# Low parts of weights over the raw tiles in place, 2048 columns at once, with other scheduling priorities

## The chip, the cores and the metric

The kernel runs on one core of one Trainium2 chip. The metric is the device time of one execution in microseconds (us); the time of a kernel is the median of several runs. The engines are named as in the profile: PE (TensorE, matmuls; PEld is its weight load), DVE (VectorE), ACT (ScalarE), POOL (GpSimd) and SP (SyncE, which issues most DMAs).

## The reference

One layer of a hybrid trunk for 256 positions and a model width of 2048, all in fp32. A normalised input is projected 13312 columns wide; the columns feed three branches of width 1024 (a spatial-gating MLP, an S5 state-space layer with a GLU, and a cross-attention into 256 memory rows) and three sets of merge gates.

```python
def hybrid_layer(x, mem, ...):
    h = rms_norm(x, pre_g)
    proj = h @ w_in
    a_u, a_v, a_g, b_x, b_g, x_q, x_g, gate_logits = jnp.split(proj, splits, axis=-1)
    y_a = spatial_gating(a_u, a_v, sg_ln_g, sg_ln_b, sg_w, sg_b) * jax.nn.silu(a_g)
    y_b = s5_branch(b_x, a_re, a_im, log_dt, b_re, b_im, c_re, c_im, d, glu_w, glu_b) * jax.nn.silu(b_g)
    y_x = memory_cross_attention(x_q, rms_norm(mem, mem_g), xa_wk, xa_wv) * jax.nn.silu(x_g)
    ys = jnp.stack([y_a, y_b, y_x], axis=2)
    branch = jnp.einsum('bsnc,ncd->bsnd', ys, w_branch)
    gates = jax.nn.sigmoid(gate_logits.reshape(bsz, seq, N_BRANCH, D_MODEL))
    merged = jnp.sum(gates * branch, axis=2)
    out = merged @ w_out
    return x + rms_norm(out, post_g)
```

## The kernel before

**Weights.** All large products go through PE in fp32r, with each fp32 number split in two: a high part (the number cast to fp32r) and a low part (what is left of it). A product is then high·high, low·high and high·low. The weights come as 160 blocks of 128 x 2048 fp32, 1 MB each. `load` (L76) issues one DMA on SP into a tile of the pool `rawp`, which has three. `split` (L85) takes half a block, 1024 columns: `halves` (L81) gives it one of four tiles of the pool `hip`, with room for 1024 high and 1024 low columns, and `split_to` (L91) has ACT cast the high part (L92) and DVE subtract it from the raw numbers (L93). So a block takes two casts and two subtractions, and its raw tile is free when the second subtraction is done.

**Matmuls.** `cm_mm` (L172) holds the weights stationary and gives channel-major results: for each 128 columns of a block one matmul of 512 columns with the high part (L175) and one of 256 with the low part (L174; L177 for the first of a group, behind the high one). `tm_mm` (L179 to L182) moves the weights, 512 columns at a time, three matmuls each (high, low, high). `cm_block` (L210) and `tm_quarter` (L218) run one block, `cm_pairs` (L234) runs blocks in pairs into one PSUM tile of the pool `accp`.

**Stages.** The first eight pieces of `start` (L250 to L272) hold x transposed and the first 512 columns of w_bx; then come four w_bx blocks of the S5 branch, the queries (w_xq), the memory's keys and values (wk, wv), the gates of the branches, and `merge` (L780), which runs for each branch over four column groups: four blocks of w_gate, a sigmoid into a tile `sg` of the pool `wk` (L785), two blocks of w_br. The GLU (L910 to L925) multiplies four blocks and writes `yB`, which the S5 branch's merge reads. `w_out` and `w_out3` (L977 to L1019) project the result; L1024 to L1042 normalise, add the residual and write `y_out`. The last `w_out3` block's first half is split into tiles of the pool `s5p`.

**What sets the order.** PE runs in program order, written out by hand. ACT, DVE, POOL and SP are ordered by the scheduler of the framework by priority, which falls in program order; `tc.high_priority(offset=n)` moves what is issued inside it n places ahead. Splits, and the normalisation of memT (`mem_half`), go ahead by AHEAD = 250. After every half block `pump` (L186) lets small background generators run on: those of `bg[2]` (`rms_row` L290, attention, layer norm and the like) a step each, and the S5 layer's main one (`bg[0]`) by credits. Their steps have BEHIND = 0, no shift. In `rms_row` the row factors are turned into a broadcast `bc_x` through a diagonal tile `dg` (L305), a matmul (L312) and an ACT copy (L315), and then multiplied onto the tiles U and X (L330). `fold_u` (L341) adds the two halves of a PSUM tile into U or X with an ACT copy (L342) and a DVE addition (L343). In attention the scores `sc` (L717) are reduced (L722, L723), turned into exponentials `p` on ACT (L726), scaled on DVE (L730, L732) and transposed on PE (`tp`, L738). The S5 layer's products and scans are L374 and L606, its small exponent tables `E` are built at L377.

Of the kernel before, what the change touches and what calls it, by code (L numbers as in the profile page):

```python
# [18 lines left out]
P = 128  # L19
# [11 lines left out]
PI2_2 = 0.0019340515136718750  # L31
PI2_3 = 2.0 * math.pi - PI2_1 - PI2_2
RND = 12582912.0
AHEAD = 250
BEHIND = 0
NWARM = 8
CM_OFF = 352 // 4
RT = (0.66, 0.8, 0.47, 0.62, 0.58, 0.55, 1.32)
GELU_S = 2.0 * math.sqrt(2.0 / math.pi)
GELU_C = 0.044715  # L40
# [3 lines left out]
def trunk(ctx: ExitStack, tc: tile.TileContext, I, out):  # L44
    nc = tc.nc
    v, a, g, pe = nc.vector, nc.scalar, nc.gpsimd, nc.tensor

    xp = ctx.enter_context(tc.tile_pool(name="xp", bufs=1))
    xv = xp.tile([P, T + 48], F32, name="xv")
    const = ctx.enter_context(tc.tile_pool(name="const", bufs=1))  # L50
    big = ctx.enter_context(tc.tile_pool(name="big", bufs=1))
    rawp = ctx.enter_context(tc.tile_pool(name="rawp", bufs=3))
    hip = ctx.enter_context(tc.tile_pool(name="hip", bufs=4))
    wk = ctx.enter_context(tc.tile_pool(name="wk", bufs=2))
    s5p = ctx.enter_context(tc.tile_pool(name="s5p", bufs=2))
    s5c = ctx.enter_context(tc.tile_pool(name="s5c", bufs=1))
# [19 lines left out]
    def load(src):  # L76
        t = rawp.tile([P, 2048], F32, tag="raw", name=nm("raw"))
        nc.sync.dma_start(out=t, in_=src)
        return t

    def halves(off):  # L81
        t = hip.tile([P, 2 * 1024 + 128], F32R, tag="hl", name=nm("hl"))
        return t[:, off:off + 1024], t[:, off + 1024:off + 2048]

    def split(src, off=0):  # L85
        hi, lo = halves(off)
        with tc.high_priority(offset=AHEAD):
            split_to(hi, lo, src)
        return hi, lo

    def split_to(hi, lo, src):  # L91
# [116 lines left out]
    rate = {"cm": 0.62, "tm": RT[6]}  # L208

    def cm_block(ps, raw, hl, mm_=cm_mm):  # L210
        for hf in range(2):
            wh, wl = split(raw[:, hf * 1024:(hf + 1) * 1024], CM_OFF)
            for k in range(8):
                kk = hf * 8 + k
                mm_(ps, wh[:, k * P:(k + 1) * P], wl[:, k * P:(k + 1) * P], hl[kk], kk == 0, kk == 15)
            pump(rate["cm"])

    def tm_quarter(acc, raw, hl, kq, nk):  # L218
        for hf in range(2):
            wh, wl = split(raw[:, hf * 1024:(hf + 1) * 1024])  # L220
            for k in range(2):
                kk = kq * 4 + hf * 2 + k
                sl = slice(k * 512, (k + 1) * 512)
                for tb in range(2):
                    tm_mm(acc[tb], wh[:, sl], wl[:, sl], hl[kk], tb, kk == 0, kk == nk - 1)
            pump(rate["tm"])
# [130 lines left out]
    cm_block(ps[:, 1], load(I["w_bx"][3]), xhl)  # L357
# [419 lines left out]
    def merge(n, yhl, sink):  # L777
        for c in range(4):
            rate["tm"] = RT[6] + (0.33, 0.13, 0.0, 0.0)[c] * (n == 2)
            G = acc_tile()  # L780
            for kq in range(4):
                tm_quarter([G[:, 0], G[:, 1]], load(I["w_gate"][n, c, kq]), xhl, kq, 16)
            assert not bg[2]
            Bp = acc_tile()
            sg = wk.tile([P, 2, 512], F32, tag="w0", name=nm("g"))  # L785
            for tb in range(2):
                a.activation(out=sg[:, tb], in_=G[:, tb], func=AF.Sigmoid, scale=rstd_x[:, tb:tb + 1])
            for kq in range(2):
                tm_quarter([Bp[:, 0], Bp[:, 1]], load(I["w_br"][n, c, kq]), yhl, kq, 8)
            sink(c, sg, Bp)  # L790
# [118 lines left out]
        yB += [s5p.tile([P, 2, T], F32R, tag=tag, name=nm("yB"), bufs=n) for _ in range(n)]  # L909
    for bp in range(4):  # L910
        ps = acc_tile()
        raw = load(I["glu"][bp])
        for b in range(2):
            wh, wl = split(raw[:, b * 1024:(b + 1) * 1024], CM_OFF)
            for k in range(8):
                cm_mm(ps[:, b], wh[:, k * P:(k + 1) * P], wl[:, k * P:(k + 1) * P], ygl[k], k == 0, k == 7)
        t = fold(ps, None)
        for i in range(2):
            a.activation(out=t[:, i, :], in_=t[:, i, :], func=AF.Sigmoid, bias=glu_b[:, 2 * bp + i:2 * bp + i + 1])
        b = slice(2 * bp, 2 * bp + 2)  # L920
        v.tensor_tensor(out=t, in0=t, in1=u[:, b, :], op=ALU.mult)
        v.tensor_tensor(out=t, in0=t, in1=sb[:, b, :], op=ALU.mult)
        for i in range(2):
            d = yB[2 * bp + i]
            split_to(d[:, 0], d[:, 1], t[:, i])  # L925
# [63 lines left out]

    acc = acc_tile()  # L990
    for kh in range(2):
        raw = load(I["w_out3"][0, kh])
        for hf in range(2):
            wh, wl = split(raw[:, hf * 1024:(hf + 1) * 1024])
            for k in range(4):
                for tb in range(2):
                    tm_k(acc[:, tb, 0:T], wh[:, k * T:(k + 1) * T], wl[:, k * T:(k + 1) * T], kh * 8 + hf * 4 + k, tb)
# [7 lines left out]

    wks = []
    for kh in range(2):
        raw = load(I["w_out3"][1, kh])
        for hf in range(2):
            src = raw[:, hf * 1024:(hf + 1) * 1024]  # L1010
            if kh == 0 and hf == 0:
                for i in range(2):
                    wh = s5p.tile([P, 512], F32R, tag="s", name=nm("wh"), bufs=4)
                    wl = s5p.tile([P, 512], F32R, tag="s", name=nm("wl"), bufs=4)
                    split_to(wh, wl, src[:, i * 512:(i + 1) * 512])
                    wks += [(wh[:, k * T:(k + 1) * T], wl[:, k * T:(k + 1) * T]) for k in range(2)]
            else:
                wh, wl = split(src)
                wks += [(wh[:, k * T:(k + 1) * T], wl[:, k * T:(k + 1) * T]) for k in range(4)]  # L1019
# [116 lines left out]
```

## Time and profile before

| | us |
|---|---|
| median of 3 runs | 913.08 |
| lowest, highest run | 912.48, 913.41 |
| the profiled execution | 913.93 |
| its span | 912.2 |
| DVE subtractions of splits (L93, 128x1024), 319 of 1220 ns | 388.1 |
| ACT casts of splits (L92, 128x1024), 319 of 1044 ns | 331.3 |

The profile is of one execution. Its page gives busy times by engine, and the trace behind it answers further views: what an engine waited for, a timeline of instructions with the idle time before each and what ended it, groups of instructions by line and form, and busy time in windows. A row of the timeline reads: start, duration, engine, line, operation, written tile <- read tiles, shape, count. Numbers of buffers are left out of names, so `hl` is any tile of `hip`, and `raw` any raw tile.

### The profile page before, as it was taken

How to read it: one execution, taken by the hardware profiler on the slowest of the kernel's cores; microseconds unless marked ns; L12 is line 12 of the kernel's file. 1: busy time of each engine (PE TensorE's matmuls, PEld its weight loads, DVE VectorE, ACT ScalarE, POOL GpSimd, SP SyncE). 2: the span in 40 equal slices, each digit the busy share in tenths (PEclk: the TensorE clock that was granted, in tenths of full speed). 3: DMA queues.
4: the chain of work that ended last, by engine and by line, in shares of the span. 5: the costliest groups of instructions: out<-in, count | busy, mean ns of one | idle time of the engine just before them, and what ended most of it. 6: DMA issues, size and time to landing. Idle time of an engine off the chain costs nothing.

```text
span 912.2 us, 12951 instructions
## 1 busy us (share of the span) xinstructions
PE 899.3 (99%) x4864; PEld 798.4 (88%) x4864; DVE 751.5 (82%) x1172; ACT 562.6 (62%) x962; POOL 49.8 (5%) x78
## 2 busy tenths in 40 slices
PE   8999999999999999999999999999999999999996
PEld 6999898889888888889989888889988889998896
DVE  6899967976779999899779998999889647876554
ACT  7585755855558677774456667767656546544452
POOL 1000000100001111110000010101000000000000
PEclk9999999999999999999999999999999999999999
DMA  9887665555455656665645656565655755557542
GB/s 337 312 311 294 226 231 194 202 193 191 154 205 176 242 187 227 231 212 207 231 167 186 221 203 212 190 213 203 231 190 194 258 195 203 211 185 277 194 175 93
DMA packets 32575, 195.30 MB, mean 214 GB/s; under 512 B 4224, under 2 KB 6528, under 8 KB 10752
## 3 DMA queue, kind: packets, MB, share of 16 engines
q1 hardware_dynamic: 28000, 186.08, 56.6%
q0 software_dynamic: 3936, 6.16, 3.1%
q10 hardware_dynamic: 576, 2.23, 0.6%
q8 instruction: 38, 0.62, 0.3%
q14 instruction: 25, 0.20, 0.1%
HBM read 190.39 MB, written 2.10 MB: 211 GB/s over the span
## 4 chain that ended last, share of the span: by engine, by line
PE 86%; DVE 9%; ACT 1%; DMA 1%; issue 1%; SPq 0%; DVEq 0%; ACTq 0%
PE acc L180 19%; PE acc L181 19%; PE acc L182 19%; PE acc L175 17%; PE acc L174 8%; DVE hl L93 4%; PE y L630 1%; ACT hl L92 1%; PE po L748 1%; DMA M<-memT 1%; DMA st<-start 1%; PE bu L568 1%; DVE q L374 1%; PE sc L717 1%; DVE tS L377 1%
## 5 line engine op out<-in xcount | busy, mean ns | idle before, releaser
L93 DVE TENSOR_TENSOR hl<-raw,hl 128x1024 fp32r<-128x1024 f32 x319 | 388.1, 1220 | 120.4 <-ACT hl L92 118.5
L92 ACT CAST hl<-raw 128x1024 fp32r<-128x1024 f32 x319 | 331.3, 1044 | 221.8 <-PE acc L182 139.1
L175 PE MATMUL acc<-x,hl 128*128 128x512 f32 x736 | 241.2, 382 | 0.0
L174 PE MATMUL acc<-x,hl 128*128 128x256 f32 x690 | 189.4, 274 | 2.6 <-DVE hl L93 2.6
L180 PE MATMUL acc<-hl,x 128*128 128x512 f32 x448 | 171.4, 383 | 0.0
L181 PE MATMUL acc<-hl,x 128*128 128x512 f32 x448 | 169.8, 379 | 0.0
L182 PE MATMUL acc<-hl,x 128*128 128x512 f32 x448 | 169.8, 379 | 0.0
L175 PEld LDWEIGHTS acc<-x,hl 128*128 128x128 f32 x736 | 136.8, 189 | 18.0 <-ACT hl L92 0.6
L174 PEld LDWEIGHTS acc<-x,hl 128*128 128x128 f32 x690 | 132.3, 192 | 4.5 <-DVE hl L93 3.2
L180 PEld LDWEIGHTS acc<-hl,x 128*128 128x128 f32 x448 | 84.7, 189 | 13.7 <-issue 2.5
L182 PEld LDWEIGHTS acc<-hl,x 128*128 128x128 f32 x448 | 84.7, 189 | 12.0
L181 PEld LDWEIGHTS acc<-hl,x 128*128 128x128 f32 x448 | 84.7, 189 | 11.3
L180 PE MATMUL acc<-hl,H 128*128 128x512 f32 (+1 forms) x224 | 83.6, 373 | 0.0
L181 PE MATMUL acc<-hl,H 128*128 128x512 f32 (+1 forms) x224 | 83.2, 372 | 0.0
L182 PE MATMUL acc<-hl,H 128*128 128x512 f32 (+1 forms) x224 | 83.2, 372 | 0.0
L175 PE MATMUL acc<-H,hl 128*128 128x512 f32 x192 | 62.6, 382 | 0.0
L539 POOL DMA_DIRECT2D B<-sb x30 | 25.4, 848 | 440.9 <-ACT B L534 409.4
L174 PE MATMUL acc<-H,hl 128*128 128x256 f32 x176 | 48.2, 274 | 0.2 <-DVE hl L93 0.2
L180 PEld LDWEIGHTS acc<-hl,H 128*128 128x128 f32 x224 | 42.4, 189 | 5.7 <-issue 0.4
L182 PEld LDWEIGHTS acc<-hl,H 128*128 128x128 f32 x224 | 42.4, 189 | 5.6
L181 PEld LDWEIGHTS acc<-hl,H 128*128 128x128 f32 x224 | 42.4, 189 | 5.3
L374 DVE TENSOR_TENSOR p<-bu,E 128x512 f32<-128x512 f32 x64 | 41.4, 684 | 1.7 <-PE bu L568 1.6
(256 smaller groups left out, 1217.7 us busy)
## 6 DMA issues: line engine op xcount, KB each, us to landing
raw<-w_gate SPq DMA_DIRECT2D x48, 1024.0 KB, 4.8
raw<-w_br SPq DMA_DIRECT2D x24, 1024.0 KB, 4.8
raw<-w_out SPq DMA_DIRECT2D x16, 1024.0 KB, 4.7
raw<-w_xq SPq DMA_DIRECT2D x8, 1024.0 KB, 5.2
raw<-wk SPq DMA_DIRECT2D x8, 1024.0 KB, 4.7
raw<-wv SPq DMA_DIRECT2D x8, 1024.0 KB, 4.9
raw<-w_xg SPq DMA_DIRECT2D x8, 1024.0 KB, 4.7
raw<-w_av SPq DMA_DIRECT2D x8, 1024.0 KB, 4.8
```

The source lines that it names most:

```text
L92: a.copy(out=hi, in_=src)
L93: v.tensor_tensor(out=lo, in0=src, in1=hi.bitcast(F32), op=ALU.subtract)
L174: pe.matmul(ps[:, 0:T], lhsT=wl, rhs=hl.moving(0), start=False, stop=False)
L175: pe.matmul(ps, lhsT=wh, rhs=hl.moving_both(), start=first, stop=last)
L180: pe.matmul(ps, lhsT=hl.stationary(0, tb), rhs=two(wh), start=first, stop=False)
L181: pe.matmul(ps, lhsT=hl.stationary(0, tb), rhs=two(wl), start=False, stop=False)
L182: pe.matmul(ps, lhsT=hl.stationary(1, tb), rhs=two(wh), start=False, stop=last)
L374: v.tensor_tensor(out=o, in0=i0, in1=i1, op=op)
L377: v.scalar_tensor_tensor(out=o, in0=i0, scalar=s, in1=i1, op0=o0, op1=o1)
L539: g.dma_start(out=B4[64:P].bitcast(F32), in_=rw[64:P], accum_op=ALU.add)
L568: pe.matmul(bu[:, ri, :], lhsT=B4[:, ri, :], rhs=two(U4), start=True, stop=True)
L630: pe.matmul(ps[32 * j:32 * j + 32, :], lhsT=cbt[:, cb * 4 + j, ri, :], rhs=ss[j][:, ri, :], start=ri == 0, stop=ri == 1, tile_position=(0, ...
```

## The change

- **Raw tiles.** Four tiles of 2176 fp32 columns lie at fixed addresses (`raws`), and the same memory is also named as fp32r (`lows`). `load` takes them in turn and returns the raw slice, the low slice over it, and its offset.
- **Splits.** `split` works on a whole block: two ACT casts of 1024 columns into one high tile of 2048 (`hip` has three such tiles now), then one DVE subtraction of 2048 columns, which writes the low part over the raw numbers. A raw tile is thus in use until PE has read its low part. Matmuls and the places of `pump` stay.
- **Priorities.** AHEAD goes from 250 to 100. Each step of the small background generators, and the GLU's epilogue, go ahead by URGENT = 400. The S5 layer's main generator has no shift, as before.
- **Around it.** The first pieces of `start` use the raw tiles, so that the first w_bx block has a free one. `sg` of `merge` moves from the pool `wk` to slots (X0 for the first merge, H0 otherwise). The last `w_out3` block is split like the others.

```diff
-AHEAD = 250
+AHEAD = 100
+URGENT = 400
+NRAW = 4
+RW = 2048 + 128
+    raws = [nc.alloc_sbuf_tensor_at(f"raw{i}", [P, RW], F32, offset=at0 + i * RW * 4).ap() for i in range(NRAW)]
+    lows = [nc.alloc_sbuf_tensor_at(f"low{i}", [P, RW], F32R, offset=at0 + i * RW * 4).ap() for i in range(NRAW)]
-    rawp = ctx.enter_context(tc.tile_pool(name="rawp", bufs=3))
-    hip = ctx.enter_context(tc.tile_pool(name="hip", bufs=4))
+    hip = ctx.enter_context(tc.tile_pool(name="hip", bufs=3))
...
+    def load(src, off=0):
+        i, sl = next_raw(), slice(off, off + 2048)
+        nc.sync.dma_start(out=raws[i][:, sl], in_=src)
+        return raws[i][:, sl], lows[i][:, sl], off
...
+    def split(raw):
+        src, lo, off = raw
+        hi = high(off)
         with tc.high_priority(offset=AHEAD):
-            split_to(hi, lo, src)
+            for hf in range(2):
+                sl = slice(hf * 1024, (hf + 1) * 1024)
+                a.copy(out=hi[:, sl], in_=src[:, sl])
+            v.tensor_tensor(out=lo, in0=src, in1=hi.bitcast(F32), op=ALU.subtract)
         return hi, lo
...
-                c = next(gen, "end")
+                with tc.high_priority(offset=URGENT):
+                    c = next(gen, "end")
...
     def cm_block(ps, raw, hl, mm_=cm_mm):
-        for hf in range(2):
-            wh, wl = split(raw[:, hf * 1024:(hf + 1) * 1024], CM_OFF)
-            for k in range(8):
-                kk = hf * 8 + k
-                mm_(ps, wh[:, k * P:(k + 1) * P], wl[:, k * P:(k + 1) * P], hl[kk], kk == 0, kk == 15)
-            pump(rate["cm"])
+        wh, wl = split(raw)
+        for k in range(16):
+            mm_(ps, wh[:, k * P:(k + 1) * P], wl[:, k * P:(k + 1) * P], hl[k], k == 0, k == 15)
+            if k % 8 == 7:
+                pump(rate["cm"])
...
-            sg = wk.tile([P, 2, 512], F32, tag="w0", name=nm("g"))
+            if c == 0:
+                sgs = slot("X0" if n == 2 else "H0", [P, 2, 2, 512])
+            sg = sgs[:, c % 2]
```

How the change moves instructions is shown at three places. The first is ACT and DVE at the first two w_bx blocks. ACT before, from the end of `start`:

```order
L92 CAST hl_371<-raw_369 128x1024
L92 CAST hl_390<-raw_369 128x1024
L342 COPY U_129<-acc_130 128x512
L342 COPY U_129<-acc_131 128x512
L92 CAST hl_415<-raw_413 128x1024
L92 CAST hl_434<-raw_413 128x1024
```

ACT of the change, at the same place:

```order
L107 CAST hl_372<-raw_58 128x1024 x2
L365 COPY U_133<-acc_134 128x512
L365 COPY U_133<-acc_135 128x512
L107 CAST hl_413<-raw_55 128x1024 x2
```

DVE of the change, at the same place:

```order
L108 TENSOR_TENSOR low_62<-raw_58,hl_372 128x2048
L366 TENSOR_TENSOR U_133<-acc_134,U_133 128x512
L366 TENSOR_TENSOR U_133<-acc_135,U_133 128x512
L108 TENSOR_TENSOR low_59<-raw_55,hl_413 128x2048
```

The U copies stand between the same two blocks on ACT; on DVE one subtraction of 2048 columns stands where two of 1024 stood.

The second place is DVE during the keys (wk), at the products with bc_x. Before:

```order
L305 TENSOR_SCALAR dg_1524<-ident,sm_1489 128x128 x2
L93 TENSOR_TENSOR hl_1223<-raw_1198,hl_1223 128x1024
L343 TENSOR_TENSOR M_81_1020<-acc_1022,M_81_1020 128x512
L330 TENSOR_TENSOR U_129<-U_129,bc_x 128x512 x3
L93 TENSOR_TENSOR hl_1253<-raw_1251,hl_1253 128x1024
L330 TENSOR_TENSOR U_129<-U_129,bc_x 128x512
L330 TENSOR_TENSOR X_39_551<-X_39_551,bc_x 128x512 x2
L93 TENSOR_TENSOR hl_1276<-raw_1251,hl_1276 128x1024
L330 TENSOR_TENSOR X_39_551<-X_39_551,bc_x 128x512 x2
```

DVE of the change, where `low_62` is the low part of the block that was `raw_1251` before:

```order
L108 TENSOR_TENSOR low_61<-raw_57,hl_1156 128x2048
L400 SCALAR_TENSOR_TENSOR E_1583<-E_1583,pwr,t_1654 128x2x64
L328 TENSOR_SCALAR dg_1463<-ident,sm_1428 128x128 x2
L353 TENSOR_TENSOR U_133<-U_133,bc_x 128x512 x4
L353 TENSOR_TENSOR X_29_541<-X_29_541,bc_x 128x512 x4
L108 TENSOR_TENSOR low_62<-raw_58,hl_1206 128x2048
L366 TENSOR_TENSOR M_55_986<-acc_988,M_55_986 128x512
```

The eight products stand together ahead of one low part, where they were spread between three halves.

The third place is DVE at the first head's softmax (the reduce of `sc`, the reciprocal and the scaling of `p`). Before:

```order
L606 SCALAR_TENSOR_TENSOR p_262_2365<-s5r,p_261_2364 128x256 x2
L374 TENSOR_TENSOR p_261_2364<-p_262_2365,E_1855 128x512
L93 TENSOR_TENSOR hl_2012<-raw_2010,hl_2012 128x1024
L722 TENSOR_REDUCE sm_1950<-sc_1926 128x2
L377 SCALAR_TENSOR_TENSOR E_2362<-E_2362,pwr,t_2558 128x2x64
L723 TENSOR_SCALAR sm_1950<-sm_1950 128x2
L374 TENSOR_TENSOR s_2563<-p_262_2365,E_1855 128x512
L374 TENSOR_TENSOR s_2563<-p_261_2364,s_2563 128x512
L93 TENSOR_TENSOR hl_2037<-raw_2010,hl_2037 128x1024
L730 RECIPROCAL sm_1951<-sm_1951 128x2
L732 TENSOR_SCALAR p_1954<-p_1954,sm_1951 128x256 x2
```

DVE of the change:

```order
L108 TENSOR_TENSOR low_60<-raw_56,hl_1923 128x2048
L745 TENSOR_REDUCE sm_1865<-sc_1844 128x2
L400 SCALAR_TENSOR_TENSOR E_2256<-E_2256,pwr,t_2400 128x2x32
L746 TENSOR_SCALAR sm_1865<-sm_1865 128x2
L629 SCALAR_TENSOR_TENSOR p_187_2259<-s5r,p_186_2258 128x256 x2
L397 TENSOR_TENSOR p_186_2258<-p_187_2259,E_1776 128x512
L753 RECIPROCAL sm_1866<-sm_1866 128x2
L397 TENSOR_TENSOR s_2445<-p_187_2259,E_1776 128x512
L755 TENSOR_SCALAR p_1869<-p_1869,sm_1866 128x256 x2
L400 SCALAR_TENSOR_TENSOR E_2256<-E_2256,pwr,t_2440 128x2x64
L397 TENSOR_TENSOR s_2445<-p_186_2258,s_2445 128x512
L108 TENSOR_TENSOR low_61<-raw_57,hl_1973 128x2048
```

The reduce stands ahead of the S5 scans (two in a row) and one product, where it stood behind them, and the reciprocal and the scaling stand ahead of the next low part, where they stood behind the next half's.

More of the change, by code (lines that the diff above doesn't have):

```diff
@@ L46, in trunk @@
     v, a, g, pe = nc.vector, nc.scalar, nc.gpsimd, nc.tensor
+    at0 = nc.sbuf_base
+    nc.alloc_sbuf_tensor("arena", [P, NRAW * RW + 128], F32)
+    at0 += (320 - at0) % 512
+    raws = [nc.alloc_sbuf_tensor_at(f"raw{i}", [P, RW], F32, offset=at0 + i * RW * 4).ap() for i in range(NRAW)]
+    lows = [nc.alloc_sbuf_tensor_at(f"low{i}", [P, RW], F32R, offset=at0 + i * RW * 4).ap() for i in range(NRAW)]
     xp = ctx.enter_context(tc.tile_pool(name="xp", bufs=1))
@@ L74, in small, with next_raw, high @@
         return const.tile(shape, dt, tag=s, name=s)
[L76 to L79, printed above, removed]
-    def halves(off):
[L82 to L86, printed above, removed]
+    turn = [0]
+    def next_raw():
+        turn[0] += 1
+        return (turn[0] - 1) % NRAW
+    def load(src, off=0):
+        i, sl = next_raw(), slice(off, off + 2048)
+        nc.sync.dma_start(out=raws[i][:, sl], in_=src)
+        return raws[i][:, sl], lows[i][:, sl], off
+    def high(off):
+        return hip.tile([P, RW], F32R, tag="hl", name=nm("hl"))[:, off:off + 2048]
+    def halves(off):
+        t = high(off)
+        return t[:, 0:1024], t[:, 1024:2048]
+    def split(raw):
+        src, lo, off = raw
+        hi = high(off)
         with tc.high_priority(offset=AHEAD):
-            split_to(hi, lo, src)
+            for hf in range(2):
+                sl = slice(hf * 1024, (hf + 1) * 1024)
+                a.copy(out=hi[:, sl], in_=src[:, sl])
+            v.tensor_tensor(out=lo, in0=src, in1=hi.bitcast(F32), op=ALU.subtract)
         return hi, lo
@@ L117, in trunk, with raw_piece @@
     const.tile([P, 32], F32, name="vpad")
-    first = rawp.tile([P, 2, 768], F32, tag="raw", name="first", padded_shape=[P, 2, 1024])
+    def raw_piece():
+        return raws[next_raw()][:, 0:1536].rearrange("p (q n) -> p q n", q=2)
+    first = raw_piece()
     nc.sync.dma_start(out=xv, in_=I["xvecs"])
@@ L210, in cm_block @@
     def cm_block(ps, raw, hl, mm_=cm_mm):
-        for hf in range(2):
-            wh, wl = split(raw[:, hf * 1024:(hf + 1) * 1024], CM_OFF)
-            for k in range(8):
-                kk = hf * 8 + k
-                mm_(ps, wh[:, k * P:(k + 1) * P], wl[:, k * P:(k + 1) * P], hl[kk], kk == 0, kk == 15)
-            pump(rate["cm"])
-    def tm_quarter(acc, raw, hl, kq, nk):
[L219 to L226, printed above, removed]
+        wh, wl = split(raw)
[3 more added lines that the diff above has]
+                pump(rate["cm"])
+    def tm_quarter(acc, raw, hl, kq, nk):
+        wh, wl = split(raw)
+        for k in range(4):
+            kk = kq * 4 + k
+            sl = slice(k * 512, (k + 1) * 512)
+            for tb in range(2):
+                tm_mm(acc[tb], wh[:, sl], wl[:, sl], hl[kk], tb, kk == 0, kk == nk - 1)
+            if k % 2:
+                pump(rate["tm"])
     def fold(ps, bc):
@@ L237, in cm_pairs @@
             for b in range(2):
-                cm_block(ps[:, b], load(src[2 * bp + b]), hl, mm_)
+                cm_block(ps[:, b], load(src[2 * bp + b], CM_OFF), hl, mm_)
             evac(bp, ps)
@@ L253, in trunk @@
         elif pc < 3:
-            raw = rawp.tile([P, 2, 768], F32, tag="raw", name=nm("st"), padded_shape=[P, 2, 1024])
+            raw = raw_piece()
         else:
@@ L345, in trunk @@
     b45 = [bup.tile([P, 512], F32, tag="bu", name=f"bx{i}") for i in (4, 5)]
-    cm_block(b45[0], load(I["w_bx"][0]), xhl)
+    cm_block(b45[0], load(I["w_bx"][0], CM_OFF), xhl)
     for i in range(2):
         fold_u(u[:, 2 * i:2 * i + 2, :], acc0[i])
-    cm_block(b45[1], load(I["w_bx"][1]), xhl)
+    cm_block(b45[1], load(I["w_bx"][1], CM_OFF), xhl)
     ps = acc_tile()
-    cm_block(ps[:, 0], load(I["w_bx"][2]), xhl)
+    cm_block(ps[:, 0], load(I["w_bx"][2], CM_OFF), xhl)
     for i in range(2):
@@ L356, in trunk @@
         nc.sync.dma_start(out=Cin[i], in_=I["s5c"][:, i])
-    cm_block(ps[:, 1], load(I["w_bx"][3]), xhl)
+    cm_block(ps[:, 1], load(I["w_bx"][3], CM_OFF), xhl)
     fold_u(u[:, 6:8, :], ps)
@@ L911, in trunk @@
         ps = acc_tile()
-        raw = load(I["glu"][bp])
+        gh, gw = (z.rearrange("p (b n) -> p b n", b=2) for z in split(load(I["glu"][bp], CM_OFF)))
         for b in range(2):
-            wh, wl = split(raw[:, b * 1024:(b + 1) * 1024], CM_OFF)
+            wh, wl = gh[:, b], gw[:, b]
             for k in range(8):
                 cm_mm(ps[:, b], wh[:, k * P:(k + 1) * P], wl[:, k * P:(k + 1) * P], ygl[k], k == 0, k == 7)
[L917 to L925, printed above, removed]
+        with tc.high_priority(offset=URGENT):
+            t = fold(ps, None)
+            for i in range(2):
+                a.activation(out=t[:, i, :], in_=t[:, i, :], func=AF.Sigmoid, bias=glu_b[:, 2 * bp + i:2 * bp + i + 1])
+            b = slice(2 * bp, 2 * bp + 2)
+            v.tensor_tensor(out=t, in0=t, in1=u[:, b, :], op=ALU.mult)
+            v.tensor_tensor(out=t, in0=t, in1=sb[:, b, :], op=ALU.mult)
+            for i in range(2):
+                d = yB[2 * bp + i]
+                split_to(d[:, 0], d[:, 1], t[:, i])
     yBs = [Plain(d, True) for d in yB]
@@ L991, in trunk @@
     for kh in range(2):
[L992 to L997, printed above, removed]
+        wh, wl = split(load(I["w_out3"][0, kh]))
+        for k in range(8):
+            for tb in range(2):
+                tm_k(acc[:, tb, 0:T], wh[:, k * T:(k + 1) * T], wl[:, k * T:(k + 1) * T], kh * 8 + k, tb)
     for tb in range(2):
@@ L1007, in trunk @@
     for kh in range(2):
[L1008 to L1019, printed above, removed]
+        wh, wl = split(load(I["w_out3"][1, kh]))
+        wks += [(wh[:, k * T:(k + 1) * T], wl[:, k * T:(k + 1) * T]) for k in range(8)]
     at = [bup.tile([P, 512], F32, tag="bu", name=nm("oacc")) for _ in range(2)]
```

## The prediction

> **What bounds the kernel now.** I read the page's first part, then PE's waits, then PE's timeline for its pace, then the engines by stage.
>
> ```profile
> span 912.2 us, 12951 instructions
> PE 899.3 (99%) x4864; PEld 798.4 (88%) x4864; DVE 751.5 (82%) x1172; ACT 562.6 (62%) x962; POOL 49.8 (5%) x78
> ...
> PE acc L174 <- DVE hl L93: 2.7, 3, 1.5
> PE wps L245 <- POOL wz L242: 1.4, 1, 1.4
> PE tp L738 <- DVE p L732: 0.8, 1, 0.8
> ```
>
> PE is idle for 912.2 − 899.3 = 12.9 us. The waits (in total, times, longest) hold 4.9 of it: 2.7 for low parts of splits, 1.4 ahead of the first matmul, 0.8 for the attention's p. The other 8.0 lie behind PE's last matmul. Busy PE time is modelled, so the pace is read from starts:
>
> ```profile
> 99.78 0.38 PE L175 MATMUL acc<-H,hl 128*128 128x512 f32 x1
> 100.34 0.38 PE L174 MATMUL acc<-H,hl 128*128 128x256 f32 x1 [0.17 <-DVE hl L93]
> ...
> 189.72 0.38 PE L175 MATMUL acc<-x,hl 128*128 128x512 f32 x1
> 190.86 0.36 PE L738 MATMUL tp<-ident,p 128*128 128x128 f32 x1 [0.76 <-DVE p L732]
> ...
> 243.76 0.38 PE L180 MATMUL acc<-hl,x 128*128 128x512 f32 x1
> 243.98 0.38 PE L181 MATMUL acc<-hl,x 128*128 128x512 f32 x1
> 244.19 0.38 PE L182 MATMUL acc<-hl,x 128*128 128x512 f32 x1
> ...
> 903.99 0.28 PE L182 MATMUL oacc<-hl,X 128*128 128x256 f32 x1
> ```
>
> At 243.76 a 512-column matmul costs 0.22 us from start to start, and nothing waits. So the gap at 99.78 costs 0.56 − 0.22 = **0.34 us**, and the one at 189.72 costs 1.14 − 0.22 = **0.92 us**. The rest of the 2.7, about 2.5 us in two waits, is in the first 11 us, behind the first pieces of start. The stages, as window, length and busy time (PE, PEld, DVE, ACT):
>
> ```profile
> 30.00:106.00 76.00, 75.83 (x463) 69.06 (x462) 73.20 (x235) 51.68 (x87) 2.97 (x7) 1.00 0.76 280
> ...
> 156.00:200.00 44.00, 43.24 (x231) 38.70 (x230) 40.73 (x63) 32.62 (x69) 4.72 (x7) 1.00 0.57 202
> 200.00:280.00 80.00, 80.00 (x427) 70.88 (x426) 58.16 (x76) 45.99 (x74) 2.87 (x4) 1.00 0.52 181
> ```
>
> DVE is 96% and 93% busy in the two stages where PE waits for it, and even there PE lacks 0.17 and 0.76 us. The clock is 1.00 throughout. Time taken off DVE is therefore worth at most these waits; the matmuls, the same ones in the same order, keep their time.
>
> **The change, part by part.** The sum stands against the profiled execution, 913.93 us, of which 912.2 is the span; the median, 913.08, lies 0.85 below it, and I carry the difference over.
>
> *One subtraction of 2048 columns.* The groups by form:
>
> ```profile
> L93 DVE TENSOR_TENSOR hl<-raw,hl 128x1024 fp32r<-128x1024 f32 x319 | 388.1, 1220 | 120.4 <-ACT hl L92 118.5
> ...
> L93 DVE TENSOR_TENSOR hl<-H,hl 128x512 fp32r<-128x512 f32 x8 | 5.5, 690 | 0.0
> ...
> L800 DVE TENSOR_TENSOR g<-acc,g 128x1024 f32<-128x1024 f32 x4 | 4.9, 1217 | 0.0
> ```
>
> 512 more columns cost 1220 − 690 = 530 ns, so 2048 columns are estimated at 1220 + 2 × 530 = 2280 ns. The ends are 2120 (columns alone, 4 × 530) and 2440 (two of the old ones). In place costs nothing extra by L800, which writes over its operand at 1217. I take 2280: 160 × 2.28 = 365 us against 388, so 23 us less on DVE, all beside PE. Directly worth: zero.
>
> *A whole block is ready later than its first half was*, by a second cast and 2280 − 1220 = 1.06 us of subtraction. The tightest place I find is the second w_bx block, whose casts stand behind two U copies that wait for PE in both kernels:
>
> ```profile
> 28.44 1.24 ACT L342 COPY U<-acc 128x512 f32<-128x512 f32 x2 [2.38 <-PE acc L175]
> 29.58 3.19 ACT L92 CAST hl<-raw 128x1024 fp32r<-128x1024 f32 x3
> ...
> 28.89 0.38 PE L175 MATMUL bx<-x,hl 128*128 128x512 f32 x1
> ...
> 33.91 0.60 PE L175 MATMUL bx<-x,hl 128*128 128x512 f32 x2
> 34.35 0.27 PE L177 MATMUL bx<-x,hl 128*128 128x256 f32 x1
> ```
>
> Two of the three casts end at 29.58 + 2.13 = 31.71, the low part at 33.99 (34.15 with 2440); PE first reads it at 34.35. So 0.2 to 0.4 us are to spare: cost zero, and at most some tenths if the operation is dearer. A block takes PE 34.13 − 28.89 = 5.24 us.
>
> *In place: a raw buffer comes free when PE is through.*
>
> ```profile
> SPq L78 <- DVE hl L93: 681.4, 139, 8.5
> ...
> raw<-w_gate SPq DMA_DIRECT2D x48, 1024.0 KB, 4.8
> ...
> M<-memT SPq DMA_DIRECT2D x2, 1024.0 KB, 7.9
> ```
>
> SP's loads wait for the subtraction now; in the change they wait for PE's last matmul of a block four earlier. That is three blocks, 15.7 us, ahead of use; 4.8 for landing, 2.1 for two casts and 2.3 for the subtraction leave 6.5, and a landing of 7.9 still leaves 3.4. Behind a waiting load on SP stand only later loads and the x, memT and mem rows, which move forward by a block at most. hi tiles are three blocks now: a cast can start two blocks, 10.5 us, ahead of use and needs 4.4 with the subtraction. Cost zero, covered by those 3.4 to 6.5 us.
>
> *Priorities.* The wait at 189.72: on DVE,
>
> ```profile
> 183.08 1.27 DVE L606 TENSOR_TENSOR_SCAN p<-s5r,p 128x256 f32<-128x256 f32 x2
> ...
> 186.13 0.68 DVE L722 TENSOR_REDUCE sm<-sc 128x2 f32<-128x512 f32 x1
> ...
> 188.95 1.23 DVE L93 TENSOR_TENSOR hl<-raw,hl 128x1024 fp32r<-128x1024 f32 x1 [0.47 <-ACT hl L92]
> ...
> 190.36 0.62 DVE L732 TENSOR_SCALAR p<-p,sm 128x256 f32<-128x256 f32 x2
> ```
>
> p's scaling stood behind a split that stood behind a cast. In the change the reduce comes ahead of the scans and one product of 0.69, so at about 184.2, and reciprocal and scaling ahead of the next low part. Its steps (0.68 and 0.16 for the reduce and its scaling, 1.27 + 0.69 for scan and product beside ACT's exponentials, then 0.16, 0.69 and 0.62) end at about 188.5; PE would come at 189.94. So the 0.92 goes, and 1.4 us stand behind it. The bounds are 0 and 0.92.
>
> The wait at 99.78 is for a second half whose subtraction was queued in the full stage; as its block now is subtracted at once, it goes: 0.34, bounds 0 and 0.34. What is late next is in that same stage:
>
> ```profile
> 103.06 0.61 PE L312 MATMUL bc<-dg,ones 128*128 128x128 f32 x4
> ...
> 106.92 0.45 ACT L315 COPY bc_x<-bc 128x256 f32<-128x256 f32 x1
> ...
> 108.89 1.88 DVE L330 TENSOR_TENSOR U<-U,bc_x 128x512 f32<-128x512 f32 x3
> ...
> 113.77 0.60 PE L175 MATMUL acc<-H,hl 128*128 128x512 f32 x2
> 114.21 0.27 PE L177 MATMUL acc<-H,hl 128*128 128x256 f32 x1
> ```
>
> The eight products with bc_x (1.88 / 3 = 0.63 each, 5.0) were spread between splits; now they stand together ahead of one low part that PE reads at 114.21. The copy of bc_x is now between the two casts of that block, the first of which can start when PE ends a block at 103.06; one cast (1.04) later it runs at 104.1 to 104.5, so the products run from 104.6 to 109.6 and the low part ends at 111.9: 2.3 us early. Cost zero.
>
> *The rest.* The GLU's epilogue is pulled forward and PE does not wait there now: zero. Start has the same order of DVE, ACT and PE: zero, with a lower bound of −2.5, the two early waits. Behind the last matmul the same chain runs: zero.
>
> **Sum:** 913.93 − 0.92 − 0.34 = 912.67 for a profiled execution, 913.08 − 1.26 = **911.8** as a median.
>
> **A rule of the skill against the change.** The Trainium skill, Perfetto Trace Analysis, Optimizing Scalar/DVE Operations, says that where these engines aren't saturated but cause bubbles elsewhere, "breaking up instructions may allow work to be completed sooner"; the change does the reverse. By it the waits would grow; the trace agrees only in so far as the two full stages hold PE's waits, and the low parts there are 0.2 to 2.3 us early in my sum.
>
> **Rivals.**
>
> *Nothing comes of it.* The waits stay, since p still waits for ACT, and the 99.78 gap turns up a block later: 913.1. For it: ACT's exponentials and casts share one queue. Against: 1.4 us of room.
>
> *Slower: the products stand ahead of the low part and start late.* DVE takes its rows in order, so the low part can't pass them. From a start at 114.21 − 2.28 − 5.0 = 106.9 on PE waits, one for one. At the old 108.89 the wait is 2.0 and the total 913.08 − 1.26 + 2.0 = 913.8; two us later still, as DVE is 96% full up to there, 4.0 and 915.8. It is slower by over 0.2% from a start at 110.0. Against: DVE has 23 us less to do, and ACT's copy no longer waits behind two casts.
>
> *Faster: start tightens too.* Order and data are as before, but two waits of 2.5 us hang there on landings and short splits; half of them gone gives 910.6, all 909.3.
>
> *Faster: PE's pace is not a floor.* If operands in other buffers let matmuls follow faster, 1 ns on each of 4864 is 4.9 us: 907. Against: the spacing is 0.22 us at 243.76, where DVE is only 73% busy (58.16 of 80) and no wait is shown. The Trainium skill, TensorE: Matmul & The Clock Gate, Back-to-back issue gap, gives about 131 ns for a sustained 512-column matmul; here the trace has 216 (243.76 to 244.19 in two), so the page's figure isn't met and the measurement decides.
>
> **How the numbers follow.** Chances: forecast 0.56 (911.2 to 912.4); nothing 0.15; late products 0.15, of which 0.05 end at 913.8 and 0.10 beyond 914.9; tighter start 0.11; pace 0.03. A measurement here can tell 0.2%, 1.83 us, from no change: below 911.25 is faster, above 914.91 slower. Of the forecast 0.07 lie below 911.25, as the runs shown spread by 0.9 us. So faster 0.07 + 0.11 + 0.03 = 0.21, slower 0.10, same 0.69. For 8 in 10 the range leaves out pace, the beyond-half of the tighter start and most of the late products: **910.2 to 914.4**.
>
> **What would show it.** PE's waits lack L738 and the 0.17, and keep the two early ones; DVE's low parts show x160 near 2280 ns and a DVE total near 728 us; SP's loads wait for PE; matmuls at 0.22 us. It is wrong if PE shows a new wait for a low part, near 34 or 114 us above all, or if the early waits or the spacing change.

## The result and the profile after

| | before | after |
|---|---|---|
| median, us (runs) | 912.95 (6) | 918.81 (6) |
| lowest, highest | 912.48, 913.99 | 918.20, 919.70 |
| span of the profiled execution | 912.2 | 918.0 |

The change made the kernel **slower by 5.9 us**: a ratio of 1.0061, 95% interval 1.005 to 1.0071. The forecast was 911.8, within 910.2 to 914.4.

The first part of the page of the change, and its group of subtractions:

```profile
span 918.0 us, 12843 instructions
...
PE 903.5 (98%) x4864; PEld 801.4 (87%) x4864; DVE 735.6 (80%) x1011; ACT 549.5 (60%) x961; POOL 49.0 (5%) x78
...
L108 DVE TENSOR_TENSOR low<-raw,hl 128x2048 fp32r<-128x2048 f32 x160 | 365.8, 2288 | 126.0 <-ACT hl L107 125.9
```

DVE has the less work that was reckoned with: 365.8 us of subtractions against 388.1, at 2288 ns each against an estimate of 2280. Yet the span grew. PE's waits say where:

```profile
PE acc L198 <- DVE M L366: 3.9, 1, 3.9
PE wps L268 <- POOL wz L265: 1.4, 1, 1.4
PE acc L200 <- DVE low L108: 0.5, 1, 0.5
PE acc L198 <- DVE f L254: 0.3, 1, 0.3
PE acc L197 <- DVE hl L113: 0.2, 1, 0.2
```

The two waits that the forecast removes are gone, the one for p and the one at 99.78. One new wait is larger than both: 3.9 us, and not for a low part but for L366, the addition in `fold_u` on M (the keys), which empties a PSUM tile that PE's next pair of blocks needs. PE's timeline at that place, and the stages around it (PEclk is the third column from the end):

```profile
113.02 0.38 PE L198 MATMUL acc<-H,hl 128*128 128x512 f32 x1
117.30 0.77 PE L198 MATMUL acc<-H,hl 128*128 128x512 f32 x1 [3.90 <-DVE M L366]
117.86 0.42 PE L200 MATMUL acc<-H,low 128*128 128x256 f32 x1
```

```profile
110.00:114.00 4.00, 3.40 (x21) 2.86 (x19) 4.00 (x8) 3.93 (x7) 0.00 (x0) 1.00 0.51 215
114.00:118.00 4.00, 0.70 (x2) 0.64 (x3) 4.00 (x4) 2.74 (x4) 0.00 (x0) 0.80 0.74 264
118.00:122.00 4.00, 4.00 (x15) 3.45 (x14) 4.00 (x4) 1.52 (x4) 0.00 (x0) 0.50 0.00 0
122.00:126.00 4.00, 4.00 (x23) 3.61 (x22) 0.68 (x2) 0.31 (x1) 0.00 (x0) 0.85 0.00 0
126.00:130.00 4.00, 4.00 (x26) 3.68 (x26) 2.27 (x1) 1.69 (x2) 0.00 (x0) 1.00 0.75 266
```

From start to start the wait is 117.30 − 113.02 − 0.22 = 4.06 us. Behind it PE is slow: 15 matmuls in the four us from 118, where 26 run from 126 on, at a granted clock of 0.50. At half clock 4 x (0.20 + 0.50 + 0.15) = 3.4 us of full clock are missing from 114 to 126; some 0.45 of them fall into the wait, so about **2.95 us** are lost to the clock. The wait and the slow clock are 7.0 us together, more than the whole 5.8 by which the span grew. What DVE did there:

```profile
104.68 2.29 DVE L108 TENSOR_TENSOR low<-raw,hl 128x2048 fp32r<-128x2048 f32 x1 [2.17 <-ACT hl L107]
106.89 0.35 DVE L400 SCALAR_TENSOR_TENSOR E<-E,pwr,t 128x128 f32<-128x128 f32 x1
...
109.44 2.50 DVE L353 TENSOR_TENSOR U<-U,bc_x 128x512 f32<-128x512 f32 x4 [1.82 <-ACT bc_x L338]
111.86 2.49 DVE L353 TENSOR_TENSOR X<-X,bc_x 128x512 f32<-128x512 f32 x4
114.27 2.29 DVE L108 TENSOR_TENSOR low<-raw,hl 128x2048 fp32r<-128x2048 f32 x1
116.47 0.68 DVE L366 TENSOR_TENSOR M<-acc,M 128x512 f32<-128x512 f32 x1
```

and ACT, which feeds it:

```profile
102.34 0.41 ACT L584 COPY E<-E 128x256 f32<-128x256 f32 x1 [1.82 <-DVE E L400]
102.66 1.99 ACT L107 CAST hl<-raw 128x1024 fp32r<-128x1024 f32 x2
...
107.27 0.41 ACT L584 COPY E<-E 128x256 f32<-128x256 f32 x1 [1.73 <-DVE E L400]
...
107.99 1.03 ACT L107 CAST hl<-raw 128x1024 fp32r<-128x1024 f32 x1
108.92 0.49 ACT L338 COPY bc_x<-bc 128x256 f32<-128x256 f32 x1
```

Read them together, backwards from the fold at 116.47. It stands behind the 17th block's low part (114.27), that behind eight products (109.44), and these waited for ACT's copy of bc_x (108.92). The copy stood behind a cast (107.99), the cast behind a copy of E (107.27) that waited for DVE's step on E (106.89). That step stood behind the 16th block's low part (104.68), which waited for its casts (102.66), and these stood behind the copy of E before. ACT and DVE took turns: each waited for the other across a cast of two us or a subtraction of 2.3.

The other differences in the profiled executions are small. New waits from start to start: 0.68 at 81.5 and 0.26 at 28.3, both for low parts, and 0.51 at 435.3 for an addition in `fold` (L254). Gone: the 0.92 and the 0.34. The first w_bx block begins 1.1 us earlier (27.79, was 28.89), but the early waits ahead of that (L113) are 0.2 us here and 2.6 in no_urgent, with the same code there, and 0 to 2.6 us over all the profiles of this case, so I put it down to the execution. 4.06 + 2.95 + 1.45 − 1.26 − 1.10 = 6.1, within 0.3 of 5.8.

### The profile page after: what moved, and what is told of

Read it like the earlier page. It is cut to its first block, busy times and chain, and to the rows that moved or that the text cites. A ratio compares the mean times of both kernels' runs of the same rounds, so it can differ in the third digit from the quotient of the medians.

```text
span 918.0 us, 12843 instructions
## 1 busy us (share of the span) xinstructions
PE 903.5 (98%) x4864; PEld 801.4 (87%) x4864; DVE 735.6 (80%) x1011; ACT 549.5 (60%) x961; POOL 49.0 (5%) x78
## 4 chain that ended last, share of the span: by engine, by line
PE 82%; DVE 12%; issue 2%; DMA 1%; ACT 1%; SPq 0%; DVEq 0%; ACTq 0%
PE acc L203 18%; PE acc L204 18%; PE acc L205 18%; PE acc L198 15%; PE acc L197 7%; DVE low L108 5%; ACT hl L107 1%; PE y L653 1%; DMA raw<-w_av 1%; PE po L771 1%; PE sc L740 1%; PE bu L591 1%; DVE H L192 1%; DVE p L397 1%; DMA raw<-start 1%
## 5 line engine op out<-in xcount | busy, mean ns | idle before, releaser
L108 DVE TENSOR_TENSOR low<-raw,hl 128x2048 fp32r<-128x2048 f32 x160 | 365.8, 2288 | 126.0 <-ACT hl L107 125.9
L197 PE MATMUL acc<-x,low 128*128 128x256 f32 x630 | 172.7, 274 | 0.0
L203 PE MATMUL acc<-hl,x 128*128 128x512 f32 x448 | 171.4, 383 | 0.0
L204 PE MATMUL acc<-low,x 128*128 128x512 f32 x448 | 169.8, 379 | 0.0
L205 PE MATMUL acc<-hl,x 128*128 128x512 f32 x448 | 169.8, 379 | 0.0
L198 PEld LDWEIGHTS acc<-x,hl 128*128 128x128 f32 x736 | 137.4, 190 | 19.1 <-ACT hl L112 0.7
L197 PEld LDWEIGHTS acc<-x,low 128*128 128x128 f32 x630 | 120.8, 192 | 1.2
L203 PEld LDWEIGHTS acc<-hl,x 128*128 128x128 f32 x448 | 84.7, 189 | 13.8 <-issue 2.5
L205 PEld LDWEIGHTS acc<-hl,x 128*128 128x128 f32 x448 | 84.7, 189 | 12.0
L204 PEld LDWEIGHTS acc<-low,x 128*128 128x128 f32 x448 | 84.7, 189 | 11.3
L203 PE MATMUL acc<-hl,H 128*128 128x512 f32 (+1 forms) x224 | 83.6, 373 | 0.0
L204 PE MATMUL acc<-low,H 128*128 128x512 f32 (+1 forms) x224 | 83.2, 372 | 0.0
L205 PE MATMUL acc<-hl,H 128*128 128x512 f32 (+1 forms) x224 | 83.2, 372 | 0.0
```

The lines of the kernel that those rows point to most:

```text
L108: v.tensor_tensor(out=lo, in0=src, in1=hi.bitcast(F32), op=ALU.subtract)
L197: pe.matmul(ps[:, 0:T], lhsT=wl, rhs=hl.moving(0), start=False, stop=False)
L198: pe.matmul(ps, lhsT=wh, rhs=hl.moving_both(), start=first, stop=last)
L203: pe.matmul(ps, lhsT=hl.stationary(0, tb), rhs=two(wh), start=first, stop=False)
L204: pe.matmul(ps, lhsT=hl.stationary(0, tb), rhs=two(wl), start=False, stop=False)
L205: pe.matmul(ps, lhsT=hl.stationary(1, tb), rhs=two(wh), start=False, stop=last)
```

## The experiments

Twelve kernels. Theory 1: the urgent products stand in front of the low part and of the fold on DVE. Theory 2: whole blocks in place make the splits late, whatever the priorities. Each median stands beside the kernel before in the same session (913.1 to 913.4).

| run | median, us | ratio, 95% interval |
|---|---|---|
| no_urgent | 922.69 | 1.0106 (1.0093 to 1.0120) |
| old_priorities | 921.74 | 1.0096 (1.0082 to 1.0110) |
| priorities_only | 917.25 | 1.0042 (1.0030 to 1.0055) |
| products_not_urgent | 913.50 | 1.0003 (0.9994 to 1.0012) |
| ahead_250 | 921.65 | 1.0091 (1.0077 to 1.0105) |
| two_halves | 922.19 | 1.0099 (1.0083 to 1.0114) |
| two_halves_old_priorities | 915.21 | 1.0021 (1.0012 to 1.0030) |
| two_halves_products | 915.82 | 1.0030 (1.0019 to 1.0040) |
| bc_not_urgent | 913.55 | 1.0006 (0.9997 to 1.0015) |
| bc_not_urgent_mem_by_pool | 914.87 | 1.0017 (1.0009 to 1.0026) |
| six_products | 916.88 | 1.0040 (1.0027 to 1.0052) |
| attention_urgent_only | 912.24 | 0.9988 (0.9979 to 0.9997) |

### Taking the products out of URGENT

```diff
-                mul_to(d, d, nrm[key][1])
+                with tc.high_priority(offset=-URGENT):
+                    mul_to(d, d, nrm[key][1])
```

The line serves the four products of the memory's keys with `bc_m` as well, so these lose their urgency too.

> The change with only the products with bc_x taken out of URGENT. Two of eight then stand ahead of the low part, six behind the fold. Theory 1: products from 109.4, low part to 113.0, fold to 113.7, PE would come at 113.2: a wait of about 0.5 us instead of 4.07 and no slow clock: about 912.3. Theory 2: 917 to 919.

913.50. DVE, at the same place:

```profile
109.52 1.29 DVE L354 TENSOR_TENSOR U<-U,bc_x 128x512 f32<-128x512 f32 x2 [1.82 <-ACT bc_x L338]
110.73 2.29 DVE L108 TENSOR_TENSOR low<-raw,hl 128x2048 fp32r<-128x2048 f32 x1
112.93 0.68 DVE L367 TENSOR_TENSOR M<-acc,M 128x512 f32<-128x512 f32 x1
```

The products start as late as in the change, but only two stand ahead, and the fold is done at 113.6. PE waits 0.45 us there, and the clock stays at 1.00. Moving the products alone is worth 5.3 us (918.8 to 913.5): theory 1 holds at this place. It is 1.2 us above what I expected; the profile shows 1.0 of that in a wait for a low part at 81.5, which stayed.

### The priorities alone

The kernel before, with half-block splits:

```diff
-AHEAD = 250
+AHEAD = 100
+URGENT = 400
...
-                c = next(gen, "end")
+                with tc.high_priority(offset=URGENT):
+                    c = next(gen, "end")
```

and the GLU's epilogue likewise.

> The kernel before with AHEAD = 100, URGENT = 400 alone, half-block splits. Theory 1: the eight products stand ahead of both halves of the 17th block and of the fold: products from about 108.4 to 113.4, two halves to 115.8, fold to 116.5, PE would come at 114.0: a wait of 2 to 3 us there, with the slow clock behind it up to 3 more, less 0.92 at p: 914 to 918. Theory 2: no such wait, 912 to 913.

917.25, with the wait at the place named:

```profile
106.64 2.49 DVE L332 TENSOR_TENSOR U<-U,bc_x 128x512 f32<-128x512 f32 x4
109.05 2.48 DVE L332 TENSOR_TENSOR X<-X,bc_x 128x512 f32<-128x512 f32 x4
111.46 2.35 DVE L94 TENSOR_TENSOR hl<-raw,hl 128x1024 fp32r<-128x1024 f32 x2
113.73 0.68 DVE L345 TENSOR_TENSOR M<-acc,M 128x512 f32<-128x512 f32 x1
```

PE waits for that fold until 114.56, 2.2 us. So the priorities alone cost time, without whole blocks; the products started at 106.64, 1.8 us sooner than I had put them. Not all of the 4 us is this wait: PE also waits for low parts at 421.9 and 426.4, 0.6 and 1.5 us from start to start, which I had not expected. In this profile the clock stays at 1.00, and the profiled execution is the fastest of the five (915.81; the others 916.67 to 918.21).

### No urgency, and the old priorities, with whole blocks

`URGENT = 0` in the change; and, in the second, `AHEAD = 250` too.

> The change with URGENT = 0, all else kept. Theory 1 (the urgent products with bc_x stand on DVE ahead of the 17th block's low part and of the fold that frees PE's next PSUM tile): both now stand ahead of the products, the 4.07 us wait of PE at 113 and the slow clock behind it (2.97 us) go, and the attention's wait for p (0.92) comes back: 918.8 - 7.0 + 0.9, about 912.7. Theory 2 (whole-block subtraction in place makes the splits late, whatever the priorities): the wait stays, 917 to 919.

> The change with AHEAD = 250 and URGENT = 0: whole blocks in place alone. Theory 1: no wait at 113, the wait for p back: 912 to 913. Theory 2: the wait stays, 917 to 919.

922.69 and 921.74. The wait at 113 is gone in both, as theory 1 has it, but the time is not 912.7: seven other waits have come. The wait for p, which I expected to come back, did not: in no_urgent p is ready at 191.07 and PE comes to it at 191.14. PE's waits without urgency, and DVE at the largest:

```profile
PE acc L203 <- ACT yB L112: 3.1, 1, 3.1
PE acc L197 <- DVE hl L113: 2.6, 2, 1.6
...
PE sc L740 <- ACT H L763: 1.4, 1, 1.4
PE acc L200 <- DVE low L108: 1.2, 2, 0.9
PE acc L198 <- DVE f L254: 0.9, 1, 0.9
```

```profile
786.11 0.68 DVE L254 TENSOR_TENSOR f<-acc,f 128x512 f32<-128x512 f32 x1
787.33 2.29 DVE L108 TENSOR_TENSOR low<-raw,hl 128x2048 fp32r<-128x2048 f32 x1 [0.54 <-ACT hl L107]
789.54 0.68 DVE L947 TENSOR_TENSOR f<-f,U 128x512 f32<-128x512 f32 x1
790.26 0.69 DVE L948 TENSOR_TENSOR f<-f,X 128x512 f32<-128x512 f32 x1
```

The GLU's epilogue, between two of its steps, stands behind a whole block's subtraction, and PE, which needs `yB`, waits 3.1 us. In the kernel before, with halves and without urgency, PE shows only the early waits, the 0.34 at 99.78 and the one for p. So theory 2 has a part of the truth: whole blocks delay the small work that PE waits for, and URGENT buys that back, nearly all of it: the change has none of the waits for `yB` and `H`, and products_not_urgent, in which all but the products is urgent again, is 9.2 us faster than no_urgent. The next two pairs separate the length of the subtraction from the rest.

### Two subtractions of half a block, in place

```diff
                 a.copy(out=hi[:, sl], in_=src[:, sl])
-            v.tensor_tensor(out=lo, in0=src, in1=hi.bitcast(F32), op=ALU.subtract)
+                v.tensor_tensor(out=lo[:, sl], in0=src[:, sl], in1=hi[:, sl].bitcast(F32), op=ALU.subtract)
```

once at the old priorities, once at the change's, once at the change's with the products not urgent.

> In place over four raw tiles, three high tiles, but two subtractions of 1024 columns, AHEAD = 250 and URGENT = 0. If the 8.5 us that whole blocks cost at the old priorities come from the long subtraction (other work stands behind it), they go for the most part: 913 to 915. If they come from holding raw and high tiles until PE is done: 920 to 922.

915.21: of the 8.5 us that whole blocks cost at the old priorities, 6.5 come from one long subtraction in place of two, which lasts longer and can start only when both casts are done. The other 2.0 stay with what is left of the change (raw tiles held until PE is done, three high tiles, other load order); these weren't taken apart. In the profile, PE still waits for the fold on M (1.7 in two waits), for H (0.5) and for `yB` (0.3).

> The change with two subtractions of 1024 columns in place of one of 2048, both over the raw tile, priorities as in the change. Products stand behind the first half, ahead of the second half and the fold. If the urgent products are the cause, PE still waits for the fold near 113, by 1 to 3 us as the hops between ACT and DVE are shorter: 913 to 916. If the length of the subtraction is the cause, no wait there: about 912.

922.19, a miss. DVE has 750.5 us of work again, and the products start even later, at 113.12:

```profile
113.12 2.49 DVE L353 TENSOR_TENSOR U<-U,bc_x 128x512 f32<-128x512 f32 x4
115.53 2.49 DVE L353 TENSOR_TENSOR X<-X,bc_x 128x512 f32<-128x512 f32 x4
117.94 1.22 DVE L108 TENSOR_TENSOR low<-raw,hl 128x1024 fp32r<-128x1024 f32 x1
119.07 0.68 DVE L366 TENSOR_TENSOR M<-acc,M 128x512 f32<-128x512 f32 x1
```

PE waits 6.4 us for the fold. Shorter hops between ACT and DVE, which I had counted on, did not come: there are more of them. Casts now take turns with subtractions: ACT's casts at 102.25, 107.53 and 113.24 each begin 0.03 us after a subtraction of DVE ends. So the wait at 113 does not need the long subtraction; the order is enough. Its size is another matter: priorities_only has the same priorities and also subtracts halves, but in the old tiles, and is 4.9 us faster (917.25). What is left of the change thus costs 2.0 us at the old priorities and 4.9 at its own; the turns of ACT and DVE may be the reason, but no run tests it.

> Two subtractions of 1024 columns in place, the change's priorities, products with bc_x not urgent. Fold and first half stand ahead of the products. If both causes are as said, no wait at 113, the epilogues stay early, p is in time: 911.5 to 913.

915.82, 3 us above what I expected. The large wait is gone, but PE waits twice for a fold on M (1.4 together) and by some tenths for H, f and the early splits; some of the 2.6 us over the kernel before isn't explained by the waits of the profiled execution.

### Low part or fold

`AHEAD = 250` in the change, which by the scheduler's order lets the 17th and the 18th low part stand between products and fold.

> The change with AHEAD = 250, URGENT kept. DVE then has four products, the 17th block's low part, four products, the 18th block's low part, and the fold that frees PE's PSUM tile. If PE at 113 waits for the fold: products from 109.4, low part to 114.2, products to 116.7, next low part to 119.0, fold to 119.7, a wait of about 6.4 us and a slow clock behind it of 3 us or more: about 921. If it waits for the low part alone: 1.0 us, about 913.

921.65. PE's wait was 6.0 us (6.2 from start to start), for the fold:

```profile
PE acc L198 <- DVE M L366: 6.0, 1, 6.0
```

It waits for the PSUM tile: the low part was ready 5.3 us earlier, at 114.26.

### How many products stand ahead

Only the last two of the eight are not urgent.

> The change with two of the eight products (the last two on X) not urgent. Six stand ahead of the 17th block's low part and the fold: 4.07 - 2 x 0.63 = 2.8 us of wait at 113. If the slow clock is a consequence of the length of PE's wait and sets in between 2.2 us (none in priorities_only) and 4.07 us, its 3.0 us shrink or go: 914 to 917. If it comes from something else in this stretch, it stays: about 917.5.

916.88. The wait is 2.7 us, 2.8 from start to start, as reckoned from 0.63 for each product, and the slow clock lasts half as long as in the change. Windows of this run:

```profile
114.00:118.00 4.00, 1.33 (x8) 1.01 (x8) 4.00 (x5) 3.63 (x5) 0.00 (x0) 1.00 0.74 248
118.00:122.00 4.00, 4.00 (x15) 3.46 (x15) 4.00 (x4) 1.15 (x4) 0.00 (x0) 0.57 0.04 16
122.00:126.00 4.00, 4.00 (x26) 3.68 (x25) 1.57 (x2) 2.20 (x4) 0.00 (x0) 1.00 0.26 57
```

### Removing what is left

The ACT copy of bc_x is not urgent either; then the loads of x and mem for the row norms go to POOL's queue as well.

```diff
-        a.copy(out=in_order(bc[:, 0, :]), in_=ps[:, 0:T].rearrange("p (c b) -> p c b", c=2))
+        with tc.high_priority(offset=-URGENT):
+            a.copy(out=in_order(bc[:, 0, :]), in_=ps[:, 0:T].rearrange("p (c b) -> p c b", c=2))
...
-        nc.sync.dma_start(out=r, in_=src)
+        nc.gpsimd.dma_start(out=r, in_=src)
```

> As products_not_urgent, with the ACT copy of bc_x not urgent either. The 17th block's low part and the fold now stand ahead of all eight products. The 0.45 us wait at 113.8 should go; the wait for a low part at 81.5 (1.0) stays: about 913.0. If the place of the products were not what made PE wait there, 0.45 stays: 913.5.

> As bc_not_urgent, with the four loads of x and mem for the row norms issued on POOL in place of SP. If the low part that PE waits for at 81.5 is late because the raw loads stood on SP behind the mem load, which itself waited for its tile, that wait (1.0) goes too: about 912.0. If it is late for DVE or ACT alone, it stays: about 913.0.

913.55 and 914.87. With the copy moved, the 0.45 us wait goes as expected, and 0.39 comes at 119.7. With the loads on POOL the wait near 82 goes too, but this doesn't settle its cause: the low part ends at 81.12, only 0.3 us earlier than in the change, and PE comes to it later, at 82.14. In the change its casts stood on ACT behind the squares of mem, and it then stood on DVE behind 3.3 us of small steps; on POOL the loads leave SP's queue, but ACT waits 4.1 us for mem, where it had waited 2.6. Small waits come at 104, 115 and 121 (0.34 to 0.50), the one at 29.6 grows from 0.38 to 0.71, and the time is 1.3 us longer, not 1.0 shorter: a miss. What decides at 81.5 stays open. Neither kernel is faster than the one before.

### Priority for the attention alone

The kernel before, half-block splits and AHEAD = 250 as they were:

```diff
-                c = next(gen, "end")
+                with tc.high_priority(offset=URGENT if gen.__name__ == "attn" else 0):
+                    c = next(gen, "end")
```

> The kernel before with only the steps of the attention's generators at URGENT = 400; half-block splits and AHEAD = 250 as before. If the 0.92 us wait for p was all that could be had from priorities, it goes and nothing comes in its place: about 912.3. If the steps put in front delay splits, a new wait takes its place: 913 or more.

912.24, against 913.09: a ratio of 0.9988, 0.9979 to 0.9997. The wait for p is gone and nothing came in its place:

```profile
PE wps L247 <- POOL wz L244: 1.4, 1, 1.4
PE acc L175 <- DVE hl L94: 0.9, 2, 0.8
```

It is the one version that beats both kernels, by 0.85 us over the kernel before. The 0.85 rests on the medians (11 and 15 runs): in the two profiles the early waits differ as well, 0.8 us here and 2.6 before.

## Why the prediction was wrong

**The bound** was right in that PE sets the time, but waits were not all there was to lose: "the matmuls, the same ones in the same order, keep their time" failed, by the 2.95 us of slow clock. **The subtraction** was right (2288 ns for 2280). DVE's busy time fell by 15.9 rather than 23 us. The times of its groups, added up, did fall by 24.0 (811.5 to 787.5 us), but the records of instructions that follow each other at once overlap (in the change the one from 104.68 ends at 106.97, the next starts at 106.89), and with 161 instructions fewer the overlap falls from 60.0 to 51.9 us. A duration in the profile is thus more than an instruction takes from a full engine. **The second w_bx block** was right within its tenths: the low part that came late there is the first block's, by 0.26. **Raw tiles freed by PE** at cost zero: no wait of PE in the change names a load; the 2.0 us that two_halves_old_priorities keeps over the kernel before, and the 4.9 between two_halves and priorities_only, may hold some of it. A wait at 81.5 that I had not foreseen cost 0.68 us in the change and 1.0 in products_not_urgent, where it takes back most of the 1.26 that were to be won. **The wait for p** went as forecast, with 0.6 us to spare for the 1.4 that I had reckoned (p is ready at 195.58, PE comes at 196.20), and attention_urgent_only shows it alone: 0.85 for 0.92. That it is gone from the change's profile proves little by itself, since it is gone from no_urgent too, where nothing is urgent. **The wait at 99.78** went as well, and did so in every kernel with whole blocks.

**The step that failed** is the copy of bc_x, "at 104.1 to 104.5, so the products run from 104.6 to 109.6 and the low part ends at 111.9: 2.3 us early. Cost zero." It ran at 108.92. I let its cast start when PE freed the high tile, at 103.06, and did not follow ACT's queue: between two casts stand the copies of E, and each waits for a step of DVE that stands behind a whole low part. The cast began at 107.99, 4.9 us later than I put it. This is read from the change's trace; no run moved the copies of E alone. Two prices were missing besides: the **fold**, which PE needs as much as the low part (0.7 us here, 5.3 in ahead_250), and the **clock** behind the wait (2.95 us). The fold was there to be seen: in the lists of DVE's order at the second place the addition on M stands ahead of the products before, and behind both them and the low part in the change.

**The rival** "the products stand ahead of the low part and start late" is what happened, at 0.15. It had the mechanism, the place and nearly the start (109.44; I priced 108.89 at 2.0 us of wait and 913.8). Its size was off for three reasons: PE came about 0.8 us earlier than before, the fold added 0.7, and the slow clock 2.95.

**The Trainium skill's rule** on breaking up instructions (Perfetto Trace Analysis, Optimizing Scalar/DVE Operations) got too little weight: two_halves_old_priorities gains 6.5 us over old_priorities by that edit. But at the change's priorities the same edit loses 3.4 us.

## What to carry to other kernels

Give a priority to the steps that the bounding engine waits for, one by one; here the same setting moved a short chain (p) and five us of products that PE was not waiting for, and the products cost 5.3 us where p gives back 0.85. When something is put ahead in an in-order queue, list all that PE needs from behind it, the emptying of its PSUM tiles as well as its operands, and take the start of the moved work from the whole chain of both queues that feed it, not from the buffer that comes free. A longer operation on a loaded engine saves time there and can delay the small steps behind it by more: at the old priorities whole blocks cost 6.5 us over halves, although DVE had less to do.

## What the runs showed of the hardware

A wait of PE of a few us can be followed by a stretch at half clock, which lasts in steps of about 3.4 us. The wait of 2.7 us in six_products gave one: 0.57 over the four us from 118, that is 3.4 us at 0.50. The wait of 3.9 us in the change gave two: 1.6 + 4.0 + 1.2 = 6.8 us. With 6.2 us in two_halves it was 6.8 us as well:

```profile
114.00:118.00 4.00, 0.00 (x0) 0.00 (x0) 4.00 (x8) 2.69 (x5) 0.00 (x0) 0.89 0.72 262
118.00:122.00 4.00, 2.10 (x7) 1.86 (x8) 3.42 (x6) 1.06 (x2) 0.00 (x0) 0.50 0.00 0
122.00:126.00 4.00, 4.00 (x21) 3.56 (x20) 3.05 (x3) 3.86 (x7) 0.00 (x0) 0.76 0.00 0
```

The 2.0 us in priorities_only gave none in its profile, and neither did the 3.1 us in no_urgent (clock 1.00 from 784 to 796). So the length of the wait does not decide alone; where it lies does. By the clock records of the traces, full clock begins at 4.4 to 7.3 us, at another time in each execution, and every later change of the clock lies a whole number of steps of 3.413 us behind that. In the 14 profiles each full-clock step in which PE was idle for 2.2 us or more was the last before half clock (2.4 us in six_products, 3.0 in the change, and the idle end of every kernel), and none with 1.9 us or less was. The 3.1 us of no_urgent fell on two steps, 1.3 and 1.9. After a slow step, the clock came back when PE had been busy throughout it (six_products), and stayed low for another step when PE had been idle for 0.9 us of it (the change).

In six_products the clock fell only when PE had been back at work for about a us, at the end of such a step. The Trainium skill, TensorE: Matmul & The Clock Gate, Part 1, has free-running windows of 3413 ns and half clock after an idle window: the steps agree; a wait of 2.7 us, shorter than a window, was enough here, so a window need not be idle throughout. A step costs up to 1.7 us, half of its length. So the same wait can cost a step in one execution and none in the next. The mean granted clock of each run, which a step lowers by 0.002, fits this in six_products (0.998 in its two fastest runs, 915.60 and 915.98, and 0.996 or 0.997 in the others). In priorities_only it fits the slowest run (0.995) but does not explain the rest. It is a weak sign, since the mean also holds the slow clock behind the last matmul, which differs from run to run.
